# Cross attention's queries as seven products of quarter blocks, with three heads' outputs through DRAM

## The chip, the cores and the metric

The kernel runs on one core of a Trainium2 chip. Times are device microseconds of one execution; a kernel's time is the median of several. TensorE (PE) multiplies, VectorE (DVE), ScalarE (ACT) and GpSimd (POOL) work on tiles in on-chip memory, and SyncE (SP) issues all the transfers.

## The reference

One decoder layer on 1024 tokens of width 1024: a mixer (mLSTM and forgetting attention), cross attention into 256 memory tokens with 4 heads of 256, and a feed-forward block of width 4096. The part that matters here:

```python
def cross_attention(h, memn, w_q, w_kv, w_o):
    q = (h @ w_q).reshape(B, S, X_HEADS, X_DH)
    k, v = jnp.split(memn @ w_kv, 2, axis=-1)
    ...
    s = jnp.einsum('bqhd,bmhd->bhqm', q, k, preferred_element_type=jnp.float32) * (X_DH ** -0.5)
    p = jax.nn.softmax(s, axis=-1)
    o = jnp.einsum('bhqm,bmhd->bqhd', p.astype(v.dtype), v).reshape(B, S, D)
    return o @ w_o

x = x + jnp.concatenate([ml_out, fx_out], axis=-1) @ w_out[l]
x = x + cross_attention(rmsnorm(x, ln_x[l]), rmsnorm(mem, ln_mem[l]), w_xq[l], w_xkv[l], w_xo[l])
u = jax.nn.relu(rmsnorm(x, ln2[l]) @ w_ff1[l])
x = x + (u * u) @ w_ff2[l]
```

## The kernel before

**Layout and precision.** Activations are kept transposed: a tile has 128 of the 1024 features on its partitions and 512 tokens (one half, `hf` 0 or 1) on its free axis. A value goes to TensorE as two parts in float32r: `split(hi, lo, src, scale)` has ScalarE write `hi` (lines 134 and 137) and VectorE the rest `lo` (lines 135 and 138). `mm3` (lines 186 to 188) multiplies with three matmuls, lo x hi, hi x lo and hi x hi, into one PSUM bank. A full product of one weight tile with one half of the activations is 8 feature tiles x 3 = 24 matmuls of 512 columns.

**Order of work.** The source is written in program order. A planner then places each engine's instructions: by its own estimate of when each is ready it takes the first ready one in program order, and allots the buffers. So an engine's list differs from the source, but once it is laid down, each engine works through it in order. SP issues transfers from one such list. `issue_after` puts a transfer behind a named one. Buffers have names and counts: `act` (7 tiles of 8 x 512), `w4` (5 of 1024), `z4` (2), `wr` (2 raw weight tiles), `wh` and `wl` (3 each, cut weights), small `r_a` to `r_y` (1 or 2 each), and PSUM banks `sc` (3), `mm`, `m2`, `ov` (1 each) and `tp` (2).

**Closing the mixer.** The output projection of the mixer was mostly done during forgetting attention and lies in DRAM as `x1d`. `full_sink` (line 1119) finishes it: per output tile n and half hf, 9 matmuls, then VectorE adds the bank to the piece of `x1d` (line 1124), the sum goes back to `x1d`, is cut with the gain of the next norm into `h2[hf]` (line 1126), and its square (ScalarE, line 222) is added up by GpSimd (line 226). The order is n 0 to 3 of half 0, n 0 to 3 of half 1, then 4 to 7 likewise. The norm's factor per token (`row_second`, by `rsqrt_sums`, line 234) isn't multiplied into the queries but into the softmax: it enters as `rcol`, a scale per token, at lines 1175 and 1177.

**Cross attention.** `cross_head` (line 1151) does one head and one half: two query tiles of 24 matmuls each (banks `mm` and `m2`, weights `w_xq` loaded and cut for each half anew), cut into `q`; scores against the head's keys (`kx`, 24 matmuls of 256 columns); maximum on VectorE (line 1173), exponential on ScalarE (line 1177), division on GpSimd (line 1180); transposes (line 1185); and two output tiles with 6 matmuls each against `vx`, cut into `oh` and `ol`. The loop at line 1326 does the four heads of half 0, then those of half 1. The outputs of a half are four `act` tiles in all, both halves held.

**After it.** `first_half` (line 1317) multiplies half 0's outputs by `w_xo`; `xo_sink` (line 1299) adds `x1d`, writes `x2d`, and makes the feed-forward's input with the factor `row` (line 1306). The first feed-forward product then already works by the scheme that the change brings to the queries: `left_up` (line 1242) makes the sums of weight quarters, the rights `H` are sums of activation quarters, and `Pair.run` (line 1385) does the seven products 1, 2, 5, 6, 3, 7, 4 in three banks: a takes products 1 and 2, c takes 5 and 3, b takes 6, 7 and 4. Product 1 is copied out (line 1396) before product 2 goes on in its bank. There two pairs' products are interleaved.

Of the kernel before, what the change touches and what calls it, by code (L numbers as in the profile page):

```python
# [9 lines left out]
F32 = mybir.dt.float32  # L10
# [34 lines left out]
def hybrid_layer(ctx: ExitStack, tc: tile.TileContext, a: dict, out: bass.AP):  # L45
# [16 lines left out]
    def act(dt=F32R):  # L62
        return sb("act", [P, 8, TH], 7, dt)
# [23 lines left out]
    def ps_tile(tag):  # L87
        return psum.tile([P, 512], F32, tag=tag, name=name(tag), bufs=PBUFS[tag])
# [42 lines left out]
    def split(hi, lo, src, scale=None):  # L131

        if scale is None:
            s.activation(hi, src, AF.Copy)  # L134
            return v.tensor_tensor(out=lo, in0=src, in1=hi.bitcast(F32), op=ALU.subtract)  # L135
        else:
            s.activation(hi, src, AF.Copy, scale=scale)
            return v.scalar_tensor_tensor(out=lo, in0=src, scalar=scale, in1=hi.bitcast(F32), op0=ALU.mult, op1=ALU.subtract)
# [51 lines left out]
    def both(pair, f):  # L190
        return f(pair[0]), f(pair[1])
# [920 lines left out]
    while late:  # L1112
        late.extend(filter(None, [late.pop(0)()]))
    banks[:] = ["mm", "tp", "m2", "tp"]
    h2 = [(act(), act())]
    x1_accs = [w2("b"), w2("b")]
    mix_done = []

    def full_sink(n, hf, ps):
        hi, lo = h2[hf]  # L1120
        t = rotate("p", "d", "e")
        with tc.issue_after(last_raw[0].ins):
            load(t, x1d[hf, :, n])
        v.tensor_tensor(out=t, in0=ps, in1=t, op=ALU.add)
        done = load(x1d[hf, :, n], t)
        split(hi[:, n], lo[:, n], t, vec[:, VEC["ln_x"] + n :][:, 0:1])
        square_sum(x1_accs[hf], t, n == 0, add=g)
        if hf == 1 and n == KT - 3:
            mix_done.append(done)

    def row_second(hf):
        rsqrt_sums(x1_accs[hf], rcol[:, 4 * hf : 4 * hf + 4], 4)
        if hf:
            to_row(row, rcol, 8, rowd[2:3])

    for n0 in (0, 4):
        ws = [weights(a["w_out_b"][n0 // 2 + i], 6 * P) for i in range(2)]
        for hf in range(2):
            if len(h2) <= hf:
                h2.append((act(), act()))  # L1140
# [10 lines left out]
    def cross_head(hd, hf, oh, ol):  # L1151
        q = []
        for kk in range(2):
            t = [rotate(*tags).bitcast(F32R) for tags in ((("b",), ("c",)), (("p",), ("a", "y")))[kk]]
            for _, _, ps in proj(weights(a["w_xq"][2 * hd + kk]), h2, 1, order=[(hf, 0)], into=ps_tile(("mm", "m2")[kk])):
                split(*t, ps, 1.0 / 16.0)
            q.append(t)
        kx, vx = w4(dt=F32R), w4(dt=F32R)
        with tc.issue_after(mix_done[0].ins):
            load(kx.bitcast(F32), kxd[hd].rearrange("p e k c -> p (e k c)"))  # L1160
            load(vx.bitcast(F32), vxd[hd].rearrange("p e m c -> p (e m c)"))
        kx, vx = (t.rearrange("p (e k c) -> p e k c", e=2, k=2) for t in (kx, vx))
        vx_parts = (vx[:, 0], vx[:, 1])
        pts = [(w2("d", dt=F32R), w2("e", dt=F32R)) for _ in range(2)]
        pr = z4()[:, :T].rearrange("p (i c) -> p i c", i=4)
        den, rden, mxc = col("den", 4), col("rden", 4), col("mx", 4)
        sps = [sc().rearrange("p (i c) -> p i c", i=2) for _ in range(2)]
        for i in range(4):
            sp = sps[i // 2]
            for kk in range(2):  # L1170
                mm3(sp[:, i % 2], both(q[kk], lambda z: z[:, i * P : (i + 1) * P]), (kx[:, 0, kk], kx[:, 1, kk]), kk == 0, kk == 1)
            if i % 2:
                v.tensor_reduce(out=mxc[:, i - 1 : i + 1], in_=sp, axis=mybir.AxisListType.X, op=ALU.max, negate=True)

                v.tensor_tensor(out=mxc[:, i - 1 : i + 1], in0=mxc[:, i - 1 : i + 1], in1=rcol[:, 4 * hf + i - 1 : 4 * hf + i + 1], op=ALU.mult)
        for i in range(4):
            s.activation(pr[:, i], sps[i // 2][:, i % 2], AF.Exp, bias=mxc[:, i : i + 1], scale=rcol[:, 4 * hf + i : 4 * hf + i + 1], accum_out=den[:, i : i + 1])
        v.reciprocal(rden, den)
        for i in range(4):
            g.tensor_scalar(out=pr[:, i], in0=pr[:, i], scalar1=rden[:, i : i + 1], scalar2=1.0, op0=ALU.mult, op1=ALU.mult)  # L1180
        yield
        for m in range(2):
            ps = tp()
            for i in range(4):
                nc.tensor.transpose(ps[:, i * P : (i + 1) * P], pr[:, i, m * P : (m + 1) * P], ident)
            split(*pts[m], ps)
        for kk in range(2):
            n = 2 * hd + kk
            ov = ov_()
            for m in range(2):  # L1190
                mm3(ov, both(vx_parts, lambda z: z[:, m, kk * P : (kk + 1) * P]), pts[m], m == 0, m == 1)
            split(oh[:, n], ol[:, n], ov)

    x2d = dram.tile([P, KT // 2, 2, 2, TH], F32, name="x2d")
    ys, free = [[], []], []
# [127 lines left out]
        cut_h(c, 0, (n % 4,))  # L1323

    os_ = []
    for hf in range(2):
        oh, ol = act(), act()
        for hd in range(XH):
            steps = cross_head(hd, hf, oh, ol)
            next(steps)  # L1330
            if hf and hd == XH - 1:
                for n in range(2):
                    first_half(n)
            for _ in steps:
                pass
            if hd == hf == 0:
                row_second(1)
        os_.append((oh, ol))
    for n in range(2, KT):
        first_half(n)  # L1340
    H.update({c: h_tile() for c in ("t1", "t2")})
# [361 lines left out]
```

## Time and profile before

| | |
|---|---|
| median of 3 runs | 1522.78 us (1521.64 to 1523.9) |
| profiled execution | 1523.35 us, span 1521.6 us |
| mean granted clock of TensorE | 0.998 |
| DMA, mean over the span | 197 GB/s |
| closing the mixer (full_sink's additions) | 603 to 639 us |
| first query matmul | 635.9 us |

An instruction's row has its start, its duration, engine, line, operation, output and inputs, and the shape. Matmuls overlap, so their step is the distance of starts, not the duration. The idle time in brackets is that of the engine before the instruction, with what ended it. A group's row has the busy time, the mean in ns, and after the second bar the idle time before the group's instructions. A window's row has the busy time of each engine in that stretch with the number of instructions, the granted clock (1.00 is full), the share of time that the DMA engines were busy, and what they moved. A row of the waits has who waited for whom, the total, the count and the longest.

### The profile page before, as it was taken

How to read it: one execution, taken by the hardware profiler on the slowest of the kernel's cores; microseconds unless marked ns; L12 is line 12 of the kernel's file. 1: busy time of each engine (PE TensorE's matmuls, PEld its weight loads, DVE VectorE, ACT ScalarE, POOL GpSimd, SP SyncE). 2: the span in 40 equal slices, each digit the busy share in tenths (PEclk: the TensorE clock that was granted, in tenths of full speed). 3: DMA queues.
4: the chain of work that ended last, by engine and by line, in shares of the span. 5: the costliest groups of instructions: out<-in, count | busy, mean ns of one | idle time of the engine just before them, and what ended most of it. 6: DMA issues, size and time to landing. Idle time of an engine off the chain costs nothing.

```text
span 1521.6 us, 21977 instructions
## 1 busy us (share of the span) xinstructions
PE 1502.7 (99%) x7694; PEld 1261.5 (83%) x7694; DVE 1100.3 (72%) x1743; ACT 727.7 (48%) x1360; POOL 510.1 (34%) x543
## 2 busy tenths in 40 slices
PE   9999999999999999999999999999999999999997
PEld 9988888889999788888888877778787888888887
DVE  7766676765787786944457989898887667787665
ACT  7324343334687665644443456666664621122124
POOL 1003030413364442511110034544555265663322
PEclk9999999999999999999999999999999999999999
DMA  6322223435888886843344437776678777776623
GB/s 239 109 77 87 98 100 114 135 126 157 246 244 267 260 264 230 300 131 124 119 147 157 153 134 277 247 256 242 222 252 286 291 277 276 276 270 248 239 94 111
DMA packets 122538, 299.86 MB, mean 197 GB/s; under 512 B 13614, under 2 KB 28264, under 8 KB 115516
## 3 DMA queue, kind: packets, MB, share of 16 engines
q1 hardware_dynamic: 122428, 298.46, 57.4%
q8 instruction: 60, 0.98, 0.3%
q14 instruction: 50, 0.41, 0.1%
HBM read 199.60 MB, written 98.81 MB: 196 GB/s over the span
## 4 chain that ended last, share of the span: by engine, by line
PE 93%; DVE 3%; ACT 2%; DMA 1%; issue 1%; SPq 0%; DVEq 0%; POOLq 0%; POOL 0%; ACTq 0%
PE tp L186 8%; PE tp L187 8%; PE tp L188 8%; PE m L186 6%; PE sc L186 6%; PE m L187 6%; PE m L188 6%; PE sc L187 6%; PE sc L188 6%; PE mm L186 6%; PE mm L187 6%; PE mm L188 6%; PE ov L186 2%; PE ov L187 2%; PE ov L188 2%; PE ov L801 2%
## 5 line engine op out<-in xcount | busy, mean ns | idle before, releaser
L186 PE MATMUL tp<-act,wl 128*128 128x512 f32 (+1 forms) x440 | 172.9, 393 | 1.2 <-ACT row L1396 0.7
L187 PE MATMUL tp<-act,wh 128*128 128x512 f32 (+1 forms) x440 | 172.1, 391 | 0.0
L188 PE MATMUL tp<-act,wh 128*128 128x512 f32 (+1 forms) x440 | 171.7, 391 | 0.0
L135 DVE TENSOR_TENSOR wl<-wr,wh 128x1024 fp32r<-128x1024 f32 (+2 forms) x95 | 124.5, 1311 | 22.0 <-ACT wh L134 21.4
L134 ACT ACTIVATE wh<-wr 128x1024 fp32r<-128x1024 f32 (+2 forms) x95 | 95.6, 1007 | 75.9 <-PE tp L188 34.7
L186 PE MATMUL mm<-act,wl 128*128 128x512 f32 (+1 forms) x332 | 127.5, 384 | 0.0
L188 PE MATMUL mm<-act,wh 128*128 128x512 f32 (+1 forms) x332 | 127.3, 383 | 0.0
L187 PE MATMUL mm<-act,wh 128*128 128x512 f32 (+1 forms) x332 | 127.2, 383 | 0.0
L186 PE MATMUL m<-act,wl 128*128 128x512 f32 (+1 forms) x308 | 117.7, 382 | 0.5 <-DVE wl L135 0.5
L188 PE MATMUL m<-act,wh 128*128 128x512 f32 (+1 forms) x308 | 117.7, 382 | 0.0
L187 PE MATMUL m<-act,wh 128*128 128x512 f32 (+1 forms) x308 | 117.5, 381 | 0.0
L186 PEld LDWEIGHTS tp<-act,wl 128*128 128x128 f32 x440 | 82.6, 188 | 20.6 <-ACT row L1396 1.2
L188 PEld LDWEIGHTS tp<-act,wh 128*128 128x128 f32 x440 | 82.6, 188 | 18.9
L187 PEld LDWEIGHTS tp<-act,wh 128*128 128x128 f32 x440 | 82.7, 188 | 18.5
L186 PE MATMUL sc<-act,wl 128*128 128x512 f32 (+1 forms) x248 | 97.0, 391 | 1.0 <-DVE wl L135 1.0
L188 PE MATMUL sc<-act,wh 128*128 128x512 f32 (+1 forms) x248 | 96.7, 390 | 0.0
L187 PE MATMUL sc<-act,wh 128*128 128x512 f32 (+1 forms) x248 | 96.6, 390 | 0.0
L1467 POOL TENSOR_TENSOR z<-wr 128x256 f32<-128x256 f32 x56 | 51.7, 944 | 130.6 <-DMA wr<-w_ff2q 116.8
L134 ACT ACTIVATE wh<-z 128x1024 fp32r<-128x1024 f32 (+1 forms) x54 | 55.5, 1028 | 80.8 <-POOL z L1467 58.4
L135 DVE TENSOR_TENSOR wl<-z,wh 128x1024 fp32r<-128x1024 f32 (+1 forms) x54 | 74.3, 1376 | 7.8 <-ACT wh L134 7.6
L134 ACT ACTIVATE w<-wr 128x768 fp32r<-128x768 f32 (+2 forms) x31 | 25.5, 823 | 106.2 <-PE tp L186 33.7
L188 PEld LDWEIGHTS mm<-act,wh 128*128 128x128 f32 x332 | 62.3, 188 | 12.7
(726 smaller groups left out, 4288.4 us busy)
## 6 DMA issues: line engine op xcount, KB each, us to landing
act<-right SPq DMA_DIRECT2D x49, 1024.0 KB
right<-w SPq DMA_DIRECT2D x56, 256.0 KB
wr<-w_ff2q SPq DMA_DIRECT2D x28, 512.0 KB
right<-r_d SPq DMA_DIRECT2D x49, 256.0 KB
right<-r_e SPq DMA_DIRECT2D x49, 256.0 KB
act<-fqk SPq DMA_DIRECT2D x48, 256.0 KB
wr<-w_in SPq DMA_DIRECT2D x20, 512.0 KB
wr<-w_ff SPq DMA_DIRECT2D x20, 512.0 KB
```

The costliest lines, as they stand in the source:

```text
L134: s.activation(hi, src, AF.Copy)
L135: return v.tensor_tensor(out=lo, in0=src, in1=hi.bitcast(F32), op=ALU.subtract)
L186: nc.tensor.matmul(ps, w[1], x[0], start=first, stop=False, skip_group_check=more)
L187: nc.tensor.matmul(ps, w[0], x[1], start=False, stop=False, skip_group_check=more)
L188: nc.tensor.matmul(ps, w[0], x[0], start=False, stop=last, skip_group_check=more)
L801: nc.tensor.matmul(self.ov[:, c0:], self.fv[:, self.j], t[:, c0:], start=self.j == 0 and t is self.p[1], stop=self.last and t is self.p[0])
L1467: g.tensor_tensor(out=o, in0=x, in1=y, op=op)
```

## The change

The queries of one head are a block product: the two output tiles of the head (rows), the two halves of the 1024 input features (inner), and the two halves of the tokens (columns). Instead of eight quarter products, seven products of sums of quarters are made, each of 4 feature tiles x 3 matmuls. For this:

- `full_sink` keeps quarters in `H2` in place of `h2`: "11" (features 0 to 3, half 0), "21", "22", and the sums t1 and t2, made with `ks`, four plain tiles of 512 that hold the first operand. The quarter (features 0 to 3, half 1) itself isn't needed. `third_right` and `fourth_right` make t3 and t4 later, loading half 0's values from `x1d` again. Seven quarters, hi and lo, fill the seven `act` tiles.
- `left_query` loads a head's two weight tiles once, makes the four sums on GpSimd in the raw tiles, and cuts them in three groups, group 0 with products 1 and 2 (and 4), group 1 with 5 and 6, group 2 with 7 and 3. Groups are called five products ahead.
- `Query.run` does the seven products. `give` cuts a finished query quarter, `add` adds a bank to what was held.
- A head's two halves are attended to one behind the other (`attend`), half 1 first, but half 0 first for the last head.
- As the `act` tiles are taken, the first three heads' outputs go to DRAM (`o_out`, `od`) and come back into `os_` tiles after the last head's last product. The last head's outputs stay (`o_keep`).
- `row_second(1)` stands right behind the mixer's close; `to_row` moves behind the last head's attention. `first_half(0)` and `first_half(1)` no longer stand amid the last head's attention, but behind it. Keys and values of a head are loaded once instead of twice.

```diff
-        split(hi[:, n], lo[:, n], t, vec[:, VEC["ln_x"] + n :][:, 0:1])
+        c = ("11", "21")[up] if hf == 0 else "22"
+        if hf == 0 or up:
+            split(H2[c][0][:, k], H2[c][1][:, k], t, gain)
+        if hf == 0 and not up:
+            s.activation(ks[k], t, AF.Copy, scale=gain)
+        if hf:
+            v.scalar_tensor_tensor(out=ks[k], in0=t, scalar=gain, in1=ks[k], op0=ALU.mult, op1=ALU.subtract)
+            c = ("t1", "t2")[up]
+            split(H2[c][0][:, k], H2[c][1][:, k], ks[k])
...
-            for _, _, ps in proj(weights(a["w_xq"][2 * hd + kk]), h2, 1, order=[(hf, 0)], into=ps_tile(("mm", "m2")[kk])):
-                split(*t, ps, 1.0 / 16.0)
...
+    row_second(1)
+    X_RIGHTS = {1: "11", 2: "21", 5: "t1", 6: "t2", 3: "22", 7: "t3", 4: "t4"}
+    X_GROUP = {1: 0, 2: 0, 5: 1, 6: 1, 7: 2, 3: 2}
...
+    def left_query(hd, group):
+        if group == 0:
+            x_raws[hd] = [sb("wr", [P, 1024], 2) for _ in range(2)]
+            for e, raw in enumerate(x_raws[hd]):
+                load(raw, a["w_xq"][2 * hd + e])
...
+        split(hi, lo, (r1, r2, r1)[group])
+        if group == 0:
+            t = w4(dt=F32R)
+            h22, l22 = t[:, :TH], t[:, TH:]
+            split(h22, l22, x22)
...
+            g.tensor_tensor(out=x21, in0=x21, in1=x22, op=ALU.add)
+            g.tensor_tensor(out=x22, in0=x21, in1=x11, op=ALU.subtract)
+            g.tensor_tensor(out=x12, in0=x12, in1=x22, op=ALU.subtract)
+            g.tensor_tensor(out=x11, in0=h22.bitcast(F32), in1=x22, op=ALU.subtract)
+            g.tensor_tensor(out=x11, in0=x11, in1=l22.bitcast(F32), op=ALU.add)
...
+    def third_right(k):
+        x = rotate("p", "d", "e")
+        load(x, x1d[0, :, k])
+        v.scalar_tensor_tensor(out=x, in0=x, scalar=vec[:, VEC["ln_x"] + k :][:, 0:1], in1=ks[k], op0=ALU.mult, op1=ALU.subtract)
+        split(H2["t3"][0][:, k], H2["t3"][1][:, k], x, -1.0)
...
+        def run(self, i, l):
...
+            at_ = {1: "a", 2: "a", 5: "c", 3: "c", 6: "b", 7: "b", 4: "b"}[i]
+            if i in (1, 5, 6):
+                setattr(self, at_, ps_tile({"a": "mm", "b": "sc", "c": "m2"}[at_]))
+            ps, r = getattr(self, at_), H2[X_RIGHTS[i]]
+            for k in range(4):
+                mm3(ps, both(l, lambda t: t[:, k]), both(r, lambda t: t[:, k]), i in (1, 5, 6) and k == 0, k == 3, True)
+            if i == 1:
+                s.activation(self.p1, ps, AF.Copy)
+            elif i == 2:
+                self.give(0, 0, ps)
...
+    def o_out(n, hf, ov):
+        t = z4()[:, :T].bitcast(F32R).rearrange("p (e c) -> p e c", e=2)
+        split(t[:, 0], t[:, 1], ov)
+        for e in range(2):
+            load(od[hf, e, :, n], t[:, e].bitcast(F32))
...
+    left_query(*x_prep.pop(0))
+    H2.update({c: quarter() for c in ("t3", "t4")})
+    x_rest = [lambda k=k: third_right(k) for k in range(4)] + [lambda k=k: fourth_right(k) for k in range(4)]
+    for at, (hd, i) in enumerate(x_jobs):
+        while x_prep and x_first[x_prep[0]] <= at + 5:
+            left_query(*x_prep.pop(0))
+        for _ in range(2):
+            if x_rest:
+                x_rest.pop(0)()
+        if i == 1:
+            query = Query(hd)
+        query.run(i, x_cuts.pop((hd, i)))
+        if i != 4:
+            continue
+        if hd == XH - 1:
+            for hf in range(2):
+                os_.append((act(), act()))
+                for p_ in range(2):
+                    for n in range(0, 2 * hd, 2):
+                        load(os_[hf][p_][:, n : n + 2].bitcast(F32), od[hf, p_, :, n : n + 2])
...
+        for hf in (0, 1) if ends else (1, 0):
+            attend(hd, hf, query.q, kx, vx, o_keep if ends else o_out)
+    to_row(row, rcol, 8, rowd[2:3])
```

More of the change, by code (lines that the diff above doesn't have):

```diff
@@ L1119, in full_sink @@
     def full_sink(n, hf, ps):
-        hi, lo = h2[hf]
+        k, up = n % 4, n // 4
+        gain = vec[:, VEC["ln_x"] + n :][:, 0:1]
         t = rotate("p", "d", "e")
@@ L1132, in row_second, with quarter @@
         rsqrt_sums(x1_accs[hf], rcol[:, 4 * hf : 4 * hf + 4], 4)
-        if hf:
-            to_row(row, rcol, 8, rowd[2:3])
+    def quarter():
+        t = act()
+        return t[:, 0:4], t[:, 4:8]
     for n0 in (0, 4):
@@ new lines, in third_right, with fourth_right @@
+    def third_right(k):
[3 more added lines that the diff above has]
+        split(H2["t3"][0][:, k], H2["t3"][1][:, k], x, -1.0)
+    def fourth_right(k):
+        x = rotate("p", "d", "e")
+        load(x, x1d[0, :, 4 + k])
+        v.scalar_tensor_tensor(out=x, in0=x, scalar=vec[:, VEC["ln_x"] + 4 + k :][:, 0:1], in1=ks[k], op0=ALU.mult, op1=ALU.subtract)
+        split(H2["t4"][0][:, k], H2["t4"][1][:, k], x)
```

89 lines of the change are left out of this document (57 added, 32 removed).

## The prediction

> **What bounds the kernel now.** I read the page's first and fourth parts, then a table of 10 us windows over the stretch that changes, then the instructions of TensorE and VectorE in order of time. The page's rows:
>
> ```profile
> span 1521.6 us, 21977 instructions
> PE 1502.7 (99%) x7694; PEld 1261.5 (83%) x7694; DVE 1100.3 (72%) x1743; ACT 727.7 (48%) x1360; POOL 510.1 (34%) x543
> PE 93%; DVE 3%; ACT 2%; DMA 1%; issue 1%; SPq 0%; DVEq 0%; POOLq 0%; POOL 0%; ACTq 0%
> ```
>
> TensorE is the bound: busy 99%, and 93% of the chain that ended last. A matmul taken away is worth its whole step, as long as TensorE finds the next operands ready. The windows show how near the other engines are (columns: TensorE, weight loads, VectorE, ScalarE, GpSimd, clock, DMA share, GB/s):
>
> ```profile
> 616.00:626.00 10.00, 10.00 (x45) 8.08 (x44) 9.80 (x11) 7.11 (x12) 6.60 (x5) 1.00 0.89 285
> 626.00:636.00 10.00, 10.00 (x45) 8.04 (x44) 9.21 (x10) 6.82 (x11) 8.10 (x7) 1.00 0.76 274
> 636.00:646.00 10.00, 10.00 (x49) 8.24 (x48) 9.01 (x13) 4.99 (x7) 5.53 (x4) 1.00 0.99 354
> 656.00:666.00 10.00, 10.00 (x52) 8.29 (x51) 4.94 (x8) 5.28 (x12) 1.85 (x4) 1.00 0.35 105
> ```
>
> From 616 to 646 us, where the mixer's output is closed by full_sink, VectorE is at 9.0 to 9.8 of 10. In cross attention behind it VectorE is at half, and TensorE never waits in either. The change puts its new VectorE work in the first of these places and takes its matmuls from the second.
>
> **The matmuls.** Per head 2 tiles x 2 halves x 8 x 3 = 96 query matmuls become 7 x 4 x 3 = 84: 48 fewer in all.
>
> ```profile
> 635.88 0.39 PE L186 MATMUL mm<-act,wl 128*128 128x512 f32 x1
> 642.36 0.39 PE L186 MATMUL m<-act,wl 128*128 128x512 f32 x1
> 647.73 0.39 PE L188 MATMUL m<-act,wh 128*128 128x512 f32 x1
> 648.55 0.28 PE L188 MATMUL sc<-w,r_b 128*128 128x256 f32 x1
> 648.67 0.40 PE L186 MATMUL mm<-act,wl 128*128 128x512 f32 x1
> ```
>
> The second and third rows are the first and last of 24 matmuls of one query tile: 5.37/23 = 0.2335 us a step. So 48 x 0.2335 = 11.2 us go, and one product of 12 matmuls takes 2.80 us. The last two rows show the planner drawing the next unit's query matmul in between one unit's scores: TensorE's order is not the program's, and holes that the planner foresees get filled.
>
> **What VectorE must do before the first head's last product.** Today the first query matmul (635.88) needs only h2 of the first half, long ready. Product 6 will need t2 and product 3 "22", both from the last four sinks; products 7 and 4 need t3 and t4, made behind the sinks. VectorE's own list decides.
>
> ```profile
> L138 DVE SCALAR_TENSOR_TENSOR act<-r_p,vec,act 128x512 fp32r<-128x512 f32 x6 | 6.9, 1142 | 0.8 <-ACT act L137 0.8
> L138 DVE SCALAR_TENSOR_TENSOR act<-r_e,vec,act 128x512 fp32r<-128x512 f32 x5 | 6.6, 1318 | 1.0 <-ACT act L137 1.0
> L138 DVE SCALAR_TENSOR_TENSOR act<-r_d,vec,act 128x512 fp32r<-128x512 f32 x5 | 5.1, 1035 | 0.0
> L135 DVE TENSOR_TENSOR wl<-wr,wh 128x1024 fp32r<-128x1024 f32 x3 | 4.1, 1375 | 0.0
> L135 DVE TENSOR_TENSOR wl<-wr,wh 128x768 fp32r<-128x768 f32 x2 | 3.0, 1504 | 1.2 <-ACT wh L134 1.2
> L1124 DVE TENSOR_TENSOR r_p<-tp,r_p 128x512 f32<-128x512 f32 x3 | 2.0, 681 | 0.3 <-PE tp L188 0.3
> L226 POOL TENSOR_TENSOR r_b<-r_c,r_b 128x512 f32<-128x512 f32 x14 | 21.1, 1517 | 33.3 <-ACT r_b L222 21.6 <-ACT r_c L222 11.4
> ```
> ```profile
> 603.01 0.69 DVE L1124 TENSOR_TENSOR r_d<-tp,r_d 128x512 f32<-128x512 f32 x1 [2.25 <-PE tp L188]
> 609.45 0.74 DVE L138 SCALAR_TENSOR_TENSOR act<-r_d,vec,act 128x512 fp32r<-128x512 f32 x1
> 610.11 1.79 DVE L138 SCALAR_TENSOR_TENSOR act<-r_p,vec,act 128x512 fp32r<-128x512 f32 x1
> 641.93 0.74 DVE L138 SCALAR_TENSOR_TENSOR act<-r_p,vec,act 128x512 fp32r<-128x512 f32 x1
> ```
>
> The groups are of 603 to 643 us. The sinks' VectorE work runs from 603.0 to 642.7, 39.7 us with about 3.0 idle: 36.7 busy. A 128x512 operation on two SBUF operands steps in 0.66 us (609.45 to 610.11) when GpSimd is quiet and takes up to 1.79 beside GpSimd's L226; the sixteen L138 average 18.6/16 = 1.16. Added to this list:
> - In the sinks: 16 cuts become 28 operations (8 combinations with ks; 8 + 8 cuts of "11", "21", t1, t2; 4 of "22"). Twelve more, at 0.66 to 1.79; I take the mean beside the same L226, 1.16: 13.9 us.
> - third_right and fourth_right: 8 x (combination + cut) = 16 operations, 0.66 to 1.16. GpSimd is then in the query weights' chain (below), less dense than L226, so 0.9: 14.4 us.
> - Weights: three wide cuts (4.1 us) become four wide (5.5) and two narrow (1.4): +2.8. Product 2's cut and two bank additions, 0.68 each: 2.0. Remaining idle time 1.0.
>
> t4 is ready at 603.0 + 36.7 + 13.9 + 14.4 + 2.8 + 2.0 + 1.0 = 673.8. With all 28 new operations at 0.66 it is 664.0; with 1.79 in the sinks and 1.16 behind, 685.5.
>
> TensorE's side: six products of head 0 last from 635.9 to 652.7. What can fill in are products of the second head, whose rights are ready: two reach to 658.3, three to 661.1, five (the most ahead of t3 and t4) to 666.7. The planner lays its list by its own times, and the profile shows VectorE slower beside GpSimd; whatever the planner didn't foresee is waited out in order. I take three: 673.8 - 661.1 = **12.7 us of stall**, between 0 (all five, 664.0) and 21 (none fills in). This eats the gain.
>
> **GpSimd and queues.** left_query puts five GpSimd operations per head ahead of groups 1 and 2. Their like in the first feed-forward product, 900 to 1200 us:
>
> ```profile
> L1256 POOL TENSOR_TENSOR wr<-wr 128x512 f32<-128x512 f32 x7 | 10.3, 1475 | 22.4 <-DMA wr<-w_ff 22.4
> L1223 POOL TENSOR_TENSOR wr<-wr,wr 128x512 f32<-128x512 f32 x14 | 21.3, 1520 | 25.9 <-DVE wl L135 18.5 <-DVE r_c L135 7.2
> L1223 POOL TENSOR_TENSOR wr<-r_b,wr 128x512 f32<-128x512 f32 x7 | 12.8, 1831 | 0.0
> L1260 POOL TENSOR_TENSOR wr<-wr,r_c 128x512 f32<-128x512 f32 x7 | 14.0, 2004 | 0.5
> ```
>
> 1.5 + 2 x 1.5 + 1.8 + 2.0 = 8.3 us a head. Heads 1 to 3 have about 32 us of TensorE work each (84 x 0.2335 and two attentions of some 6.5), so it hides there; if not, 8.3 us a head would show, which I don't expect. VectorE per later head: 4 us of weight cuts, 5 additions, 4 cuts and two attentions of about 4.5, some 20 us: hidden.
>
> ScalarE gets 8 more cuts, 4 copies of ks and the eight of t3 and t4, 20 x 0.7 us, over two stretches where its row stands at 5.0 to 7.1 of 10: hidden.
>
> On SP, 8 w_xq and 8 kxd/vxd loads of 512 KB go; 8 x1d loads of 256 KB, 24 od stores of 256 KB and 12 od loads of 512 KB come. The x1d loads (2.1 MB) fall where the DMA share is 0.99: at 354 GB/s 5.9 us of transfer, but VectorE's own backlog lasts longer than that, so 0; the w_xq, kxd and vxd loads that fill that window today are fewer. The od traffic is 12.6 MB, 35 us of transfer at that rate, in a stretch where the share is 0.35: 0, hidden under four heads; with the cover gone its 6.3 MB of loads are 17.8 us. On SP a load behind a store waits for that store's data; w_xq is loaded a head ahead, so TensorE doesn't see it. Where an od store holds a z4 buffer, ScalarE's exponentials of the next half wait, and behind them on ScalarE the next head's cuts; a head of 32 us has room for that: 0. row_second and to_row are moved, not added: to_row's two transfers run under the last head's attention, and its reader L1306 comes later.
>
> **Smaller terms.** Product 2 goes on in product 1's bank and has to wait for the copy out; product 4 likewise behind 7. The feed-forward's pairs have the same dependency, with one wait in 16 pairs:
>
> ```profile
> PE tp L186 <- ACT row L1396: 0.7, 1, 0.7
> ```
>
> Eight such places: 0 to 5.6 us; the fill-ins speak for the low end: 1.0. Behind t4, VectorE still owes six operations (3.9 us) ahead of the scores while product 4 covers 2.8: 0 to 4, taken 1.5. At the end the last head's first attention has no next head beside it. Its chain, from head 0 of today:
>
> ```profile
> 657.09 0.16 DVE L1175 TENSOR_TENSOR c_mx<-c_mx,rcol 128x2 f32<-128x2 f32 x1
> 660.37 1.85 POOL L1180 TENSOR_SCALAR z<-z,c_rden 128x256 f32<-128x256 f32 x4 [15.55 <-DVE c_rden L1178]
> 677.83 1.04 PE L1185 MATMUL tp<-ident,z 128*128 128x128 f32 x8
> ```
>
> 5.1 us to the end of L1180, 1.0 of transposes, about 1.3 for the cut: 7.4. Beside it lie the other half's scores (24 steps of 0.12: 2.8) and first_half's six k from DRAM, 4.2 us for each bank. 0 (two banks) to 7.4 (od loads late); taken 1.0.
>
> **Sum**: -11.2 + 12.7 + 1.0 + 1.5 + 1.0 = +5.0 us. The profiled execution took 1523.35, span 1521.6; the median of the runs is 0.6 lower, 1522.78. Forecast 1522.8 + 5.0 = **1527.8 us**.
>
> **Rivals.**
> - *The cover holds (faster).* If the new VectorE operations cost 0.9 or less and five products of head 1 lie ahead, t4 comes at 603.0 + 36.7 + 28 x 0.9 + 5.8 = 670.7, the stall is 4.0, the sum -3.7: 1519. At 0.66 the stall is nil: 1515. For it: VectorE's row at 603.01 and the idle times show some slack, and the planner does draw matmuls forward. Against: 9.8 of 10 at 616. It decides from a stall of 4.7 us down.
> - *The od round trip is late (slower still).* Head 2's halves follow each other through two z4 buffers that also hold the stores; if its loads land after the last attention, TensorE waits up to 7.4 more and the sum is about +12: 1535. Against: head 3's 19.6 us of products lie between.
> - *The clock falls in the stall.* The end of the kernel shows the granted clock going down when TensorE pauses:
>
> ```profile
> 1513.00:1514.00 1.00, 0.00 (x0) 0.00 (x0) 0.17 (x2) 0.00 (x0) 0.71 (x1) 1.00 0.76 262
> 1514.00:1515.00 1.00, 0.57 (x3) 0.57 (x4) 0.32 (x2) 0.00 (x0) 0.00 (x0) 0.84 0.00 0
> 1515.00:1516.00 1.00, 0.45 (x3) 0.15 (x1) 0.44 (x1) 0.00 (x0) 0.00 (x0) 0.50 0.00 0
> ```
>
> If the 12.7 us come as two long gaps, and each is followed by the clock of 0.50 for as long as the profile still shows it there (some 3 us), 2 x 1.5 us come on top: 1531. Against: short pauses between products keep it up. The Trainium skill, "TensorE: Matmul & The Clock Gate", Part 1, has the rule: an idle window of about 3.4 us halves the clock, and as much activity restores it. By its figures the same two gaps would cost an estimated 3.4 us. The end of this trace agrees with the fall to 0.50; the recovery isn't shown here.
> - *The change doesn't do what it says* isn't possible for the count of matmuls; it is only a matter of when they can run.
>
> **From cases to numbers.** Forecast 0.47 (1523 to 1533), cover holds 0.30 (1514 to 1519), late round trip 0.14 (1533 to 1540), clock 0.09 (1530 to 1536). 0.2% is 3.0 us, about what can be told from no change: of the forecast's case 0.15 lies below 1525.8 and counts as same. Faster 0.30, same 0.15, slower 0.55. The range takes in both ends: 1514 to 1540.
>
> **What would show it.** 48 matmuls fewer (7646). Right: windows from 640 to 680 us with TensorE below 10.00 and VectorE at 10, TensorE's waits naming the cuts of H2 (VectorE, act), cross attention shorter otherwise. L138 beside GpSimd above 1.1 us. Wrong: no TensorE wait there, with head 1's products ahead of head 0's product 4; or waits on DMA for act from od, ahead of the first output product; or VectorE saturated in later heads too.

## The result and the profile after

The changed kernel takes 1564.41 us (median of four executions, 1562.03 to 1569.41), the kernel before 1523.34 beside it: a ratio of 1.0276, interval 1.0252 to 1.03. It is slower, as forecast, but by 41 us where 5 were forecast, and 24 us above the upper end of the range (1540). The profiled execution is the longest of the four, 1569.41 us. Its page:

```profile
span 1567.7 us, 22060 instructions
PE 1515.3 (97%) x7646; PEld 1263.9 (81%) x7646; DVE 1141.6 (73%) x1791; ACT 737.6 (47%) x1380; POOL 536.0 (34%) x563
```

The 48 matmuls are gone (7646), yet TensorE is busy for longer than before (1515.3 against 1502.7 us): many of its matmuls have become slower. The windows of the changed kernel show where (columns as in the prediction; before the change the TensorE column is full, and the clock 1.00, in all of these stages):

```profile
626.00:646.00 20.00, 14.14 (x53) 10.49 (x52) 17.94 (x16) 9.29 (x15) 17.00 (x10) 0.91 0.59 195
646.00:666.00 20.00, 16.77 (x57) 13.29 (x58) 20.00 (x25) 11.80 (x20) 11.74 (x7) 0.70 0.52 180
666.00:690.00 24.00, 20.41 (x76) 15.83 (x76) 18.50 (x26) 6.89 (x10) 8.69 (x7) 0.82 0.21 66
730.00:750.00 20.00, 16.75 (x76) 12.99 (x75) 9.05 (x15) 8.82 (x18) 1.84 (x4) 0.91 0.51 157
810.00:830.00 20.00, 16.45 (x65) 12.63 (x66) 5.16 (x11) 7.33 (x21) 3.68 (x8) 0.83 0.48 158
```

There are two regions. From 626 to 690 us, the end of full_sink and the first head, VectorE is busy for 56.4 of 64 us (all of 646 to 666) and TensorE idles 20 - 14.14 + 20 - 16.77 + 24 - 20.41 = 12.7 us; the clock falls to 0.70. From 690 to 850, the later heads, no engine is full, and TensorE still idles. The same two stretches as one row each, first the kernel before, then the changed one:

```profile
626.00:690.00 64.00, 64.00 (x329) 53.72 (x328) 38.21 (x56) 29.21 (x57) 19.30 (x19) 1.00 0.55 188
690.00:850.00 160.00, 160.00 (x778) 132.34 (x777) 93.40 (x140) 67.17 (x125) 15.45 (x24) 1.00 0.42 142
```
```profile
626.00:690.00 64.00, 51.31 (x185) 39.61 (x185) 56.45 (x65) 27.98 (x44) 37.43 (x24) 0.81 0.43 142
690.00:850.00 160.00, 140.47 (x678) 113.00 (x677) 76.21 (x121) 59.24 (x129) 25.40 (x40) 0.96 0.47 152
```

So TensorE loses 12.7 us of idle time and 0.19 x 51.3 = 9.7 us of clock in the first head, 19.5 us of idle time and 0.04 x 140.5 = 5.6 us of clock behind it. Less the 11.2 us saved that makes 36 of the 46.1 us between the two spans. The rest is a matter of counting: a matmul's end is modelled at 0.39 us and its step is 0.2335, so that each pause is counted 0.16 us short. Reckoned from the starts of all matmuls of the two traces (what each step takes over 0.2335 us, or 0.1185 at 256 columns; a step with idle time in it is a pause), pauses cost 34.6 us more than before, slow steps 16.3 and the small matmuls (transposes and sums) 6.3; these 57.2 us less 11.2 are 46.0.

The clock in the first head isn't the same in every execution. Two kernels below leave that head's products as they are (without the od traffic, and with the probabilities in r_f tiles). They idle 14.9 and 15.2 us between 626 and 690 us at a clock of 0.92: 18.8 and 19.1 us in all, where this execution, the longest of its four, loses 22.4.

What TensorE waited for, of the changed kernel (total, times, longest):

```profile
PE sc L186 <- ACT z L1266: 8.1, 6, 2.7
PE ov L186 <- DVE z L135: 4.2, 3, 1.4
PE sc L187 <- DVE act L135: 3.6, 2, 2.4
PE sc L186 <- DVE r_f L1220: 3.3, 1, 3.3
PE tp L186 <- DVE r_e L1125: 2.9, 1, 2.9
PE mm L187 <- DMA act<-od: 1.9, 1, 1.9
PE mm L186 <- DMA act<-od: 0.7, 1, 0.7
```

The first two are the later heads: matmuls into a bank of scores wait for the exponentials (L1266) to empty it, and output products wait for the cut of the output before (into z). Rows three to five are the first head and the sinks before it. The last two are the return of the outputs from DRAM, 2.6 us in all.

### The profile page after: what moved, and what is told of

It reads as the page before. It is cut to its first block, busy times and chain, and to the rows that moved or that the text cites. A ratio compares the mean times of both kernels' runs of the same rounds, so it can differ in the third digit from the quotient of the medians.

```text
span 1567.7 us, 22060 instructions
## 1 busy us (share of the span) xinstructions
PE 1515.3 (97%) x7646; PEld 1263.9 (81%) x7646; DVE 1141.6 (73%) x1791; ACT 737.6 (47%) x1380; POOL 536.0 (34%) x563
## 5 line engine op out<-in xcount | busy, mean ns | idle before, releaser
L135 DVE TENSOR_TENSOR wl<-wr,wh 128x1024 fp32r<-128x1024 f32 (+2 forms) x91 | 119.4, 1313 | 27.2 <-ACT wh L134 27.0
L134 ACT ACTIVATE wh<-wr 128x1024 fp32r<-128x1024 f32 (+2 forms) x91 | 91.2, 1004 | 90.4 <-PE sc L188 33.4
L186 PE MATMUL sc<-act,wl 128*128 128x512 f32 (+1 forms) x280 | 111.7, 399 | 5.7 <-DVE r_f L1220 3.3
L186 PE MATMUL mm<-act,wl 128*128 128x512 f32 (+1 forms) x300 | 116.0, 387 | 1.1 <-DMA act<-od 0.7
L187 PE MATMUL mm<-act,wh 128*128 128x512 f32 (+1 forms) x300 | 114.7, 382 | 1.9 <-DMA act<-od 1.9
L188 PE MATMUL mm<-act,wh 128*128 128x512 f32 (+1 forms) x300 | 114.7, 382 | 0.0
L187 PE MATMUL sc<-act,wh 128*128 128x512 f32 (+1 forms) x280 | 111.0, 396 | 3.6 <-DVE act L135 3.6
L188 PE MATMUL sc<-act,wh 128*128 128x512 f32 (+1 forms) x280 | 110.8, 396 | 0.0
L186 PE MATMUL m<-act,wl 128*128 128x512 f32 (+1 forms) x276 | 107.0, 388 | 1.5 <-DVE r_f L1220 1.0
L187 PE MATMUL m<-act,wh 128*128 128x512 f32 (+1 forms) x276 | 106.6, 386 | 0.0
L188 PE MATMUL m<-act,wh 128*128 128x512 f32 (+1 forms) x276 | 106.6, 386 | 0.0
L134 ACT ACTIVATE w<-wr 128x768 fp32r<-128x768 f32 (+3 forms) x35 | 28.1, 801 | 120.0 <-PE tp L186 33.1
L186 PEld LDWEIGHTS sc<-act,wl 128*128 128x128 f32 x280 | 53.6, 191 | 19.8 <-DVE r_f L1220 3.7
```

The source lines that it names most:

```text
L186: nc.tensor.matmul(ps, w[1], x[0], start=first, stop=False, skip_group_check=more)
L187: nc.tensor.matmul(ps, w[0], x[1], start=False, stop=False, skip_group_check=more)
L188: nc.tensor.matmul(ps, w[0], x[0], start=False, stop=last, skip_group_check=more)
```

## The experiments

Three theories stood against each other. F: the first head is held by VectorE's list. Z: the later heads are held by the two z4 tiles, which hold a half's probabilities and also stage its outputs. C: the idle time itself brings the clock down. Where no number of executions is given, a run is one execution; the changed kernel's own executions spread over 7 us, so differences of a few us between such runs aren't read. The kernel before took 1522.1 us beside the first four runs, 1522.9 beside the next four, and 1525.9 beside the last four.

**Staging in other tiles (w4).**

```diff
 def o_out(n, hf, ov):
-    t = z4()[:, :T].bitcast(F32R).rearrange("p (e c) -> p e c", e=2)
+    t = w4(dt=F32R).rearrange("p (e c) -> p e c", e=2)
```

> The outputs on their way to od are cut into w4 tiles (5 of them, 4 taken at a time by weights, keys and values) and no longer into the two z4 tiles that the softmax needs as well. Theory A, the shared z4 tiles chain each half's exponentials to the stores of the half before: the stretch 690 to 815 us loses its waits of scores on exponentials (8.1 us) and of the second output on the cut (4.2 us) with the slow clock behind them, 12 to 18 us less than the changed kernel, 1546 to 1552 us. Rival B, the whole loss is VectorE's backlog in the first head: no change beyond 3 us, 1561 to 1567 us.

1567.33 us (median of four, 1564.74 to 1569.45), ratio to before 1.0298 (1.0274 to 1.0323). The waits on z went, and others came. The largest waits of TensorE in this kernel:

```profile
PE sc L186 <- DMA w<-kxd: 12.1, 3, 4.9
PE ov L186 <- DVE w L135: 5.8, 4, 1.5
```

The keys are loaded into w4 too. With the outputs in these tiles, the keys come late. This neither bears out Z nor refutes it: it shows that the tile borrowed was needed where it was.

**Without the od traffic.**

```diff
-        for e in range(2):
-            load(od[hf, e, :, n], t[:, e].bitcast(F32))
...
-    load(os_[hf][p_][:, n : n + 2].bitcast(F32), od[hf, p_, :, n : n + 2])
+    load(os_[hf][p_][:, n : n + 2].bitcast(F32), x1d[hf, :, n : n + 2])
```

> The stores to od are left out, and the last loads read x1d instead, so three heads' outputs are wrong; the cuts into z4 stay. If it is the stores' landing that holds the z4 tiles (theory A), this gives at least what the other staging gives, 12 to 20 us less than the changed kernel, and the waits on od at the end (2.6 us) go too: 1544 to 1552 us. If it is the mere number of z4 tiles and the order of cuts, clearly less than the other staging gives. Rival B: 3 us at most, from the od waits alone.

1560.52 us: 4 less, within the spread. In this kernel TensorE still waits 7.3 us for the exponentials and 4.2 us for the cuts into z. So it isn't the landing of the stores that makes the bulk of these waits. What was left of Z was the number of tiles and their order.

**Tiles of their own for the staging.** First the kernel without t3 and t4 (products 7 and 4 use t1 and t2), which frees two act tiles, then the same with the staging in these:

```diff
-    H2.update({c: quarter() for c in ("t3", "t4")})
-    x_rest = [lambda k=k: third_right(k) for k in range(4)] + [lambda k=k: fourth_right(k) for k in range(4)]
+    H2.update({"t3": H2["t1"], "t4": H2["t2"]})
+    x_rest = []
```
```diff
+    stage = [act() for _ in range(2)]
 def o_out(n, hf, ov):
-    t = z4()[:, :T].bitcast(F32R).rearrange("p (e c) -> p e c", e=2)
+    j = (n + 1 - hf) % 2 + 2 * (1 - hf)
+    t = stage[n // 2 % 2][:, 2 * j : 2 * j + 2]
```

> t3 and t4 aren't made: products 7 and 4 of all heads use t1 and t2 instead, so the outputs mean nothing; 16 VectorE operations, 8 ScalarE cuts and 8 loads go, and two act tiles come free. Theory B, VectorE's backlog holds up the first head's products: the stall before head 0's last products goes and its slow clock, 9 to 15 us less than the changed kernel, 1549 to 1555 us. Rival C, the sinks alone are the trouble and t3 and t4 hide behind head 1's products: at most 4 us less, 1560 us and above.

> The third and fourth right sums are left out as in the kernel that took 1556.5 us, and the two 16 KB tiles that this frees stage the heads' outputs, so that the two z4 tiles hold the exponentials alone. Theory A (in the later heads two z4 tiles serve two purposes, and TensorE waits behind the exponentials): the waits of scores and of outputs on z go from 12.3 us to under 3 us, and the time falls by 8 to 14 us, to 1542-1549. Rival B (the later heads are held by VectorE, GpSimd and the single bank of the outputs): less than 3 us, 1553-1558.

Without t3 and t4: 1556.54 us, 8 less than the changed kernel, between the two theories and hardly more than the spread. With the staging moved as well: 1537.19, another 19.3 less. The row of the later heads without t3 and t4, then both rows with the staging moved:

```profile
690.00:850.00 160.00, 143.62 (x678) 113.98 (x677) 78.94 (x124) 61.40 (x126) 21.66 (x34) 0.97 0.51 166
```
```profile
626.00:690.00 64.00, 56.49 (x262) 45.31 (x261) 51.93 (x64) 29.99 (x54) 42.11 (x32) 0.95 0.37 124
690.00:850.00 160.00, 151.64 (x742) 124.55 (x741) 94.03 (x149) 68.47 (x133) 21.09 (x33) 0.98 0.56 184
```

From 690 to 850 us the idle time is 8.4 us, in place of 16.4 without t3 and t4 and 19.5 in the changed kernel; the first head, from 626 to 690 us, hardly changes (7.5 after 6.9 us, the clock 0.95 in both). Z holds, and is worth more than the 8 to 14 us that I gave it.

**The probabilities in r_f tiles.** The same cause from the other side, with nothing left out: the staging keeps z4, and the probabilities go into the two small tiles that the queries need only between products 5 and 7.

```diff
-    pr = z4()[:, :T].rearrange("p (i c) -> p i c", i=4)
+    pr = [t[:, j * NM : j * NM + NM] for t in (w2("f"), w2("f")) for j in range(2)]
```

> The exponentials go into the two r_f tiles, which the queries use only between a head's products 5 and 7, and the z4 tiles stage outputs alone; nothing is left out. Theory A (z4's two purposes cost the later heads): waits on z fall under 4 us and the time by 6 to 12 us, to 1552-1558. Rival B (any tile lent is missed elsewhere, as with the keys' tiles): the next head's products 5 and 6 wait for VectorE's additions into r_f, 1561-1568.

1545.35 us, 19.1 less, again more than expected. The first exponential of each head's first half, of the changed kernel and then of this one, shows the beat of the heads:

```profile
694.18 0.56 ACT L1266 ACTIVATE z<-sc,c_mx,rcol 128x256 f32<-128x256 f32 x1 [3.72 <-DVE c_mx L1264]
736.00 0.56 ACT L1266 ACTIVATE z<-sc,c_mx,rcol 128x256 f32<-128x256 f32 x1
775.06 0.56 ACT L1266 ACTIVATE z<-sc,c_mx,rcol 128x256 f32<-128x256 f32 x1 [0.73 <-DVE z L135]
```
```profile
688.88 0.56 ACT L1266 ACTIVATE r_f<-sc,c_mx,rcol 128x256 f32<-128x256 f32 x1 [3.01 <-DVE c_mx L1264]
695.68 0.55 ACT L1266 ACTIVATE r_f<-sc,c_mx,rcol 128x256 f32<-128x256 f32 x1
723.43 0.56 ACT L1266 ACTIVATE r_f<-sc,c_mx,rcol 128x256 f32<-128x256 f32 x1 [2.58 <-DVE c_mx L1264]
757.61 0.56 ACT L1266 ACTIVATE r_f<-sc,c_mx,rcol 128x256 f32<-128x256 f32 x1 [2.22 <-DVE c_mx L1264]
```

(In the second group, the second row belongs to the second half of the first head.) A head takes 41.8 and 39.1 us in the changed kernel, 34.6 and 34.2 here. How the shared tiles do it is seen on ScalarE in the changed kernel. The second half's scores are complete at 697.1 us, but its exponentials come directly behind the cut of the first half's second output, 25.9 us after the first half's exponentials, where the kernel with r_f tiles has 6.8 us:

```profile
719.62 0.58 ACT L134 ACTIVATE z<-ov 128x512 fp32r<-128x512 f32 x1
720.09 0.55 ACT L1266 ACTIVATE z<-sc,c_mx,rcol 128x256 f32<-128x256 f32 x1
```

So the two halves' chains (scores, exponentials, transposes, outputs) run one behind the other instead of interleaved, and the scores of the second half keep their banks meanwhile. The order stands in ScalarE's list. It is the same without the stores (cut at 715.03 us, exponentials at 715.51), so it isn't a landing that is waited for there. That the two tiles are why the planner laid the list so is inferred from the two runs that relieve them, in which the second half's exponentials come within 7 us of the first half's; the trace doesn't number the tiles.

**GpSimd's additions left out.**

```diff
-        square_sum(x1_accs[hf], t, n == 0, add=g)
+        if n == 0:
+            square_sum(x1_accs[hf], t, True, add=g)
+        else:
+            s.activation(w2("c"), t, AF.Square)
```

> The sum of squares over the feature tiles in full_sink is left out (the squares are made, GpSimd's 14 additions are not), so the norm's factor is wrong; nothing else changes. Theory B with the part that GpSimd plays in it: VectorE's operations of the sinks on two operands in on-chip memory go from about 1.2 to 1.8 us back to 0.7, VectorE is through 8 to 12 us earlier, and the first head's holes and slow clock shrink: 8 to 16 us less than the changed kernel, 1548 to 1556 us. Rival: VectorE is long because of the number of its operations, GpSimd is no part of it: at most 3 us less.

1551.75 us, 12.7 less. The groups of VectorE's combinations with ks (L1133) over 603 to 678 us, first of the changed kernel, then of this one:

```profile
L1133 DVE SCALAR_TENSOR_TENSOR w<-r_d,vec,w 128x512 f32<-128x512 f32 x3 | 5.2, 1745 | 0.0
L1133 DVE SCALAR_TENSOR_TENSOR w<-r_p,vec,w 128x512 f32<-128x512 f32 x3 | 4.3, 1432 | 0.0
L1133 DVE SCALAR_TENSOR_TENSOR w<-r_e,vec,w 128x512 f32<-128x512 f32 x2 | 2.5, 1257 | 0.0
```
```profile
L1133 DVE SCALAR_TENSOR_TENSOR w<-r_d,vec,w 128x512 f32<-128x512 f32 x3 | 2.2, 748 | 0.0
L1133 DVE SCALAR_TENSOR_TENSOR w<-r_p,vec,w 128x512 f32<-128x512 f32 x3 | 2.2, 747 | 0.0
L1133 DVE SCALAR_TENSOR_TENSOR w<-r_e,vec,w 128x512 f32<-128x512 f32 x2 | 1.5, 746 | 0.0
```

12.0 us for eight operations become 5.9. That GpSimd lengthens VectorE's list is shown, and that shortening the list shortens the kernel, as F has it. The Trainium skill, "SBUF — State Buffer", section "SBUF: two separate sides", says that VectorE's operations with two inputs in SBUF (the on-chip memory of the tiles) and GpSimd's share a port pair, which one of them holds for a whole instruction; the means of 1.26 to 1.75 us against 0.75 agree.

**The first head with eight products.** The rights needed are then 11, 21, t1 and 22 alone; t3 and t4 have until the second head. The head's weights are cut as they are, without sums.

```diff
-    x_jobs = [(hd, i) for hd in range(XH) for i in X_RIGHTS]
+    x_jobs = [(0, i) for i in range(11, 19)] + [(hd, i) for hd in range(1, XH) for i in X_RIGHTS]
+    D_RIGHTS = {11: "11", 12: "21", 13: "t1", 14: "22", 15: "11", 16: "21", 17: "t1", 18: "22"}
...
+    r = H2[D_RIGHTS[i + 11]]
...
+    if i == 0:
+        s.activation(p1, self.ps, AF.Copy)
+    elif i == 1:
+        self.give(kk, 0, self.ps)
+    elif i == 3:
+        self.add(p1, self.ps, p1)
+        self.give(kk, 1, p1)
```

> The first head's queries by eight quarter products from rights that are cut before its start (11, 21, t1, 22), in place of seven: 12 matmuls more (2.8 us), and the third and fourth right sums are not needed until the second head, some 30 us later. Theory A (the first head's stall is VectorE's list of right sums): TensorE's lost 22.6 us between 626 and 686 us come back less the 2.8: 1541-1549. Rival B (the list is late for the second head too, or the stall has another source): the loss moves to 686-730 us, and the time stays at 1556-1565.

1550.84 us, 13.6 less than the changed kernel; I expected 1541 to 1549, 15 to 23 less. Its row of the first stretch:

```profile
626.00:690.00 64.00, 56.97 (x271) 44.42 (x269) 58.33 (x79) 32.59 (x56) 36.73 (x26) 1.00 0.47 159
```

The clock is full, the idle time 7.0 in place of 12.7 us, in pauses of at most 1.8 us. VectorE is still at 58 of 64: the sinks' additional work stays, and t3 and t4 are still made in this stretch (643 to 665 us), only that nothing waits for them there.

**F and Z together, once with and once without the work.** The kernel without t3, t4 and with the act staging, and without GpSimd's additions:

> As the run with the staging in the freed tiles, and GpSimd's 14 additions of the square sums are left out too, so that the output isn't the reference's. If VectorE's list in the first head and the shared z4 tiles are the whole of the loss, little but the 48 matmuls saved (11.2 us) is left to see: 1511-1520. If the first head is held by something else as well, or the later heads are: 8 to 13 us below the run without this edit, and above 1525.

```profile
626.00:690.00 64.00, 61.53 (x301) 49.91 (x300) 48.93 (x72) 35.20 (x63) 30.64 (x25) 1.00 0.39 131
690.00:850.00 160.00, 156.47 (x755) 127.76 (x754) 98.20 (x156) 68.25 (x129) 18.91 (x29) 0.99 0.59 193
```

1522.45 us: 42 us less than the changed kernel and as long as the kernel before beside it (1522.93), and idle time falls to 2.5 and 3.5 us. It isn't 1511 to 1520: these 6.0 us (the 3.5 lie between 750 and 810 us, around the last head) and the clock (0.01 x 156 = 1.6) still eat most of what the 48 matmuls save. And this kernel leaves out work that a correct one has to do.

And the two edits that leave nothing out (eight products in the first head, probabilities in r_f):

> The two edits together that leave nothing out: eight products in the first head, and the exponentials in the r_f tiles. Alone they took 13.6 and 19.1 us off 1564.4. Theory (two separate causes, VectorE's list in the first head and the shared z4 tiles in the later ones): they add up, 1529-1535. Rival (both relieve one backlog, in the first head and what it drags along): hardly better than the better of the two, 1541-1546.

1538.8 us, above the 1529 to 1535 expected and below the rival's 1541 to 1546. It is 13.0 over the kernel before on its chip, where 13.6 + 19.1 less than 41.1 would leave 8.4. So they add up but for some 5 us (7 by the times themselves), about the spread; whether that shortfall is real stays open. Two more runs go on top of it. First another order of the products, with the additions to match, half 0 first in every head, and the tiles for the returning outputs handed out in another order (the line of the order alone is shown):

```diff
-    x_jobs = [(0, i) for i in range(11, 19)] + [(hd, i) for hd in range(1, XH) for i in X_RIGHTS]
+    x_jobs = [(0, i) for i in range(11, 19)] + [(hd, i) for hd in range(1, XH) for i in (1, 2, 6, 7, 4, 5, 3)]
```

> As the run with both edits, and in heads 1 to 3 the products in the order 1, 2, 6, 7, 4, 5, 3, which completes the first half's queries two products earlier, so that products 5 and 3 (5.6 us) can run beside that half's scores; the first half's chain comes first in every head. Theory (the last head's chain has no cover: TensorE is some 7 us short of full there between 760 and 830): 3 to 6 us less than without this order, 1524-1531. Rival (what is short there are loads, VectorE or the single bank): within 2 us.

Then, on top of that, the square sums on TensorE:

```diff
-        square_sum(x1_accs[hf], t, n == 0, add=g)
+        sq = w2("c", dt=F32R)
+        s.activation(sq, t, AF.Square)
+        nc.tensor.matmul(x1_sums[hf][:1], ones.bitcast(F32R), sq, start=n == 0, stop=n == KT - 1, skip_group_check=True)
```

> As the run with that order, and the square sums of the rows are added up by TensorE (16 matmuls of 512 columns, 3.7 us) in place of GpSimd's 14 additions of 1.5 us; nothing is left out. Theory (VectorE is slowed beside GpSimd, which cost 12.7 us in the changed kernel, and still keeps it full until 670 us with eight products in the first head): 3 to 8 us less net of the 3.7. Rival (with eight products the list is off the path): 2 to 4 us more.

1535.91 us, above the 1524 to 1531 of its theory, and 1537.87 us, 2 more, as the rival of the second had it. The order is worth 2.9 us, less than the spread. The sums on TensorE fill the first stretch from 626 to 666 us, where the run before idled 4.8 us, but the 16 matmuls cost 3.7 us, and in the row below TensorE idles 24 - 20.34 = 3.7 us, 2.4 of them at once for exponentials (2.6 us in the run before).

```profile
666.00:690.00 24.00, 20.34 (x106) 16.71 (x104) 11.18 (x22) 9.80 (x25) 8.86 (x12) 0.93 0.19 66
```

None of the versions beats the kernel before; the best that leaves nothing out is 10.1 us (0.7%) above it.

**A pause alone.** The kernel before, with three pauses on TensorE near its end, where it otherwise runs without a gap. TensorE's list is held to the program's order there, so that the pauses fall where they are put:

```diff
+    if wid == TH and n in (1, 4, 7):
+        z = [w2("f"), w2("f")]
+        s.activation(z[0], old, AF.Copy)
+        for j in range({1: 0, 4: 1, 7: 3}[n]):
+            s.activation(z[(j + 1) % 2], z[j % 2], AF.Copy)
+        nc.tensor.matmul(ps[:, :P], z[{1: 0, 4: 1, 7: 3}[n] % 2][:, :P], ident, start=True, stop=True)
...
-    ending = last_part(0, 0, TH, iter(()))
+    with in_order((mybir.EngineType.PE,)):
+        ending = last_part(0, 0, TH, iter(()))
```

> The kernel before, and nothing of the change in it: near its end, where TensorE runs its matmuls at 0.2335 us without a gap, three small matmuls are put in that wait for one, two and four ScalarE copies in a row (0.6 us each), so that TensorE idles some 1.3, 1.9 and 3.2 us. Theory (an idle TensorE alone brings the clock down): the steps behind the longer gaps double to about 0.44 us for 3 to 5 us, and the three gaps cost 4 to 7 us more than their idle time of some 6.4 us. Rival (the double steps in the first head come from what ran beside them there, VectorE, GpSimd or loads): steps of 0.2335 us right behind the gaps, and no more than the idle time.

TensorE in order of time around the first two pauses:

```profile
1465.26 0.39 PE L188 MATMUL m<-act,wh 128*128 128x512 f32 x1
1469.67 0.77 PE L186 MATMUL tp<-act,wl 128*128 128x512 f32 x1
...
1474.09 0.63 PE L187 MATMUL tp<-act,wh 128*128 128x512 f32 x1
1474.51 0.63 PE L188 MATMUL tp<-act,wh 128*128 128x512 f32 x1
...
1475.33 0.39 PE L187 MATMUL sc<-act,wh 128*128 128x512 f32 x1
1475.57 0.39 PE L188 MATMUL sc<-act,wh 128*128 128x512 f32 x1
...
1484.23 0.48 PE L186 MATMUL sc<-act,wl 128*128 128x512 f32 x1
...
1487.56 0.63 PE L187 MATMUL sc<-act,wh 128*128 128x512 f32 x1
1487.99 0.63 PE L188 MATMUL sc<-act,wh 128*128 128x512 f32 x1
```

The pauses were longer than I had reckoned, 4.2, 3.5 and 4.8 us (from start to start, less one step). Behind the first, 12 matmuls step in 0.43 us (1474.09 to 1474.51) and then at once in 0.24. The three slow stretches cost 2.6, 1.5 and 1.6 us over full steps, 5.7 in all; with 12.5 us of pause that is 18.2. The span is 1539.5 us, 17.9 more than in the trace of the kernel before (up to 1440 us the two traces hold 7269 and 7268 matmuls, so nothing else sets them apart by then); the run of the kernel before beside it, whose trace wasn't kept, was itself longer, and leaves 15.4. C holds: the matmuls behind the pauses are those of the kernel before, and only the pauses (with the copies in them) were added. The same double step stands in the changed kernel's first head, with VectorE's addition into r_f as the cause of the pause:

```profile
671.33 0.40 PE L188 MATMUL mm<-act,wh 128*128 128x512 f32 x1
675.02 0.80 PE L186 MATMUL sc<-act,wl 128*128 128x512 f32 x1 [3.29 <-DVE r_f L1220]
679.45 0.63 PE L187 MATMUL sc<-act,wh 128*128 128x512 f32 x1
679.88 0.63 PE L188 MATMUL sc<-act,wh 128*128 128x512 f32 x1
```

But a pause need not do it. The same pause at the same product, in the kernel with the probabilities in r_f tiles:

```profile
673.25 0.50 PE L186 MATMUL sc<-act,wl 128*128 128x512 f32 x1 [3.29 <-DVE r_f L1220]
673.59 0.39 PE L187 MATMUL sc<-act,wh 128*128 128x512 f32 x1
673.82 0.40 PE L188 MATMUL sc<-act,wh 128*128 128x512 f32 x1
```

In the changed kernel 15 slow steps follow at once, 2.9 us lost; here, and in the kernel without the od traffic, none; with the staging in w4 tiles they begin 1 us after the restart. Which it is changes from run to run, so a part of each first head's time is chance.

## Why the prediction was right in its sign and wrong in its size

| step, as predicted | predicted | measured |
|---|---|---|
| 48 matmuls | -11.2 | 7646 matmuls; no run shows the saving by itself |
| stall in the first head | 12.7 (0 to 21) | idle 12.7, 626 to 690 us |
| clock in the stall | a rival, 3 | 9.7 there (3.9 in two other runs), 5.6 behind it |
| z4 shared with the staging | 0 ("has room") | some 19, idle time and clock |
| od traffic | 0 | 4 or less |
| bank waits, backlog behind t4 | 1.0 + 1.5 | waits for the additions into r_f, 4.3, inside the first head's 12.7 |
| last head without cover | 1.0 (0 to 7.4) | idle 3.6, 810 to 830 us, 2.6 of it for od |

**The first head** was read rightly: VectorE's list decides. Its last cut of t4 ends at 677.4 where I had 673.8:

```profile
676.76 0.68 DVE L135 TENSOR_TENSOR act<-r_e,act 128x512 fp32r<-128x512 f32 x1
```

The eight combinations took 1.50 us each (12.0/8) against my mean of 1.16, and the sixteen operations for t3 and t4 1.11 (17.7/16) against 0.9. That the 12.7 us agree to the digit is luck; their place is another: I put them between 661 and 674, as one stall with three products of the second head drawn in. The pauses begin at 630.7 and come in seven pieces, and only one product of the second head lies ahead of the first head's product 7. The first piece has a cause that I had costed at nothing, the load of w_xq ("a head ahead, so TensorE doesn't see it"). On ScalarE of the changed kernel the weight's cut stood 4.17 us for it, with three of the sinks' cuts queued behind:

```profile
627.96 0.63 ACT L134 ACTIVATE w<-wr 128x512 fp32r<-128x512 f32 x1 [4.17 <-DMA wr<-w_xq]
```

**The clock** was a rival with 9 in 100 and 3 us. Its mechanism was right and its size wrong, as I counted two long pauses. Seven pauses between 630 and 675 us hold the clock at 0.81 over 64 us. The 3 us for which I had the clock stay down couldn't be read from the end of the trace: the clock is at 0.50 there from 1515 to 1521 us, and from 1516 us on TensorE has nothing more to do. "Short pauses between products keep it up" fell in part: pauses of 1.7 to 2.9 us brought steps of 0.43 us too, while those of at most 1.8 us in the kernel with eight products left the clock full. The Trainium skill, "TensorE: Matmul & The Clock Gate", Part 1, has windows of some 3.4 us that run freely, so that the slow stretch depends on where a pause falls in them; the three pauses at will agree with slow stretches of 5.3, 2.9 (starting 1.5 us after the restart) and 3.5 us, and so do the 3.3 us pauses with and without slow steps. By the same part of the Trainium skill the clock falls after an idle window of that length; here the pause of 2.9 us before 634.0 us was enough for some six steps of 0.43 us, and the measurement decides. Some of this clock loss lies beside VectorE's list and would have been idle time otherwise; how much wasn't separated.

**The step that failed** is "Where an od store holds a z4 buffer, ScalarE's exponentials of the next half wait ... a head of 32 us has room for that: 0". I saw the wait and weighed it by time: a head has 32 us, a chain 7. But the tiles don't delay the chain by a fixed amount. Each half uses a z4 tile three times, once for its probabilities and twice for its outputs, so two tiles serve six uses per head; the halves no longer overlap, the score banks stay occupied, and TensorE, whose list is fixed, stands in front of them. A head took 41.8 and 39.1 us, not 32. Two runs that give the probabilities or the staging tiles of their own took 19.1 and 19.3 us off. And it wasn't the store: without stores the waits stay. The rival of the late round trip named the two tiles too, but only at the end and for the loads; their wait is the 2.6 us shown above. The clock, left out of the sum and kept as a rival, is the second step that was mis-sized: with the z4 cause removed the kernel still took 1545.35 us.

**The other rivals.** The cover did not hold. Of the marks that I gave for being wrong, VectorE saturated in later heads didn't come (76 of 160 us), and the waits on od were small. Of the marks for being right, the waits on H2's cuts and VectorE at 10 came (646 to 666 us); that cross attention would otherwise be shorter didn't.

## What to carry to other kernels

When a change puts a new use on a buffer, count its uses per round and not the time that it is held: if two chains that overlapped now need the same tile in turn, the price is the overlap. Moving the use to a tile that is itself in demand only moves the wait (12.1 us on the keys here); look for a tile that is idle in that very phase. And price a stall of TensorE with the clock: here each of three pauses of some 4 us cost about 2 us more, and one of 3.3 us either 2.9 more or nothing, so work that saves 11 us of matmuls can't afford even a few pauses.

## What the runs showed of the hardware

- A pause of 3.5 to 4.8 us in an otherwise full stretch doubled the step of a 512-column matmul from 0.2335 to 0.43 us for 2.9 to 5.3 us, in one case only 1.5 us after the restart. A pause of 3.3 us at one and the same product was followed by 15 slow steps, by some from 1 us after the restart on, or, in two runs, by none.
- Executions of the changed kernel spread over 7 us (1562.0 to 1569.4), those of the kernel before over 5. The changed kernel's mean clock was 0.986 in its longest execution and 0.991 in one of the shortest; that of the kernel before was 0.997 or 0.998 in each of the executions whose clock is on record.
- VectorE operations on 128x512 with two operands in SBUF went from 0.75 us to means of 1.26 to 1.75 us beside GpSimd, while those that read a PSUM bank (L1125, L1220) stayed at 0.68 in the same stretch.
